# A layer with retention, attention and a squared-ReLU MLP: output rows normalised by a diagonal in their transposition, modulation's last quarter in two parts, h's second pairs at 2.5 steps per unit

## The chip, the cores and the metric

The kernel runs on one core of one Trainium2 chip. The metric is the device time in microseconds (us). The engines are TensorE (PE in the profile, its weight loads PEld), VectorE (DVE), ScalarE (ACT), GpSimd (POOL) and SyncE (SP), which here issues nearly all DMAs. Each engine runs its own instructions in order and waits for other engines by semaphores. A DMA queue is in order too: a transfer whose buffer isn't free yet holds up all that were issued behind it on that queue.

## The reference

One transformer layer over 2048 rows of 1024 (f32), with 256 rows of context. Cut to what matters here:

```
mod = silu(c) @ w_mod + b_mod                     # six parts of 1024
sh1, sc1, g1, sh2, sc2, g2 = split(mod, 6)
h  = rmsnorm(x, norm1_g) * (1 + sc1) + sh1
rq, rk, rv, rg, aq, ak, av = split(h @ w_in, ...)
ret = retention(rq, rk, rv, rg)                   # 4 heads of 128, both directions
att = attention(aq, ak, av, context)              # 8 heads of 64, 2 kv heads, 2304 keys
x  = x + g1 * (concat(ret, att) @ w_out)
h2 = rmsnorm(x, norm2_g) * (1 + sc2) + sh2
x  = x + g2 * (square(relu(h2 @ w_ff1)) @ w_ff2)  # 1024 -> 4096 -> 1024
out = rmsnorm(x, final_norm_g)
```

rmsnorm(x, g) is x · rsqrt(mean(x²) + 1e-6) · g over a row. The factor of norm2_g and 1 + sc2 is a number per column, and sh2 likewise; the factor rsqrt(...) is a number r per row.

## The kernel before, in words

**Precision.** The large products split f32 operands into a high and a low f16 part and multiply three times (high·high, high·low, low·high): one product is three MATMULs. Transpositions, modulation and parts of the retention are in f32.

**Start.** Modulation is made in four quarters, objects `mods[0]` to `mods[3]` of the class `Modulation` (L315 on): `load` fetches weights of a quarter ("wm"), `product(k)` multiplies two of its eight blocks of 128 rows (L341, in a PSUM tile "mpm" from a pool of two), `end` adds the bias on VectorE and turns the row into columns (L312, L344 to L347), and `shift_and_scale` makes the columns of sh1 and of the factor. The function `modulation(q, ...)` issues the products of a quarter with other work between them; `first.bound(k)` is a part of the first column block of w_in that needs the shifts. The order of calls is the order on PE.

**Middle.** The in-projections follow, and from about 630 us attention, written as a schedule by hand: `on(k, phase, fn)` puts a call at step k in one of eleven phases ("pe", "early", "late", "dma" and so on), and one loop issues everything in the order of step and phase. There are 32 groups of 18 steps. Per step the engines work on scores (L209, L210) and maxima (pieces L172, DVE's L185), exponentials (ACT L215), the split of the probabilities in high (ACT L219) and low parts (POOL L226 or DVE L228; tile "plo"), and values (L242 and L243). Retention (f32 matmuls at L1375, VectorE and ScalarE work) runs in between.

**Output tiles.** Sixteen tiles of 128 rows, t from 15 down to 0, one every 35 steps, each by `output_tile(t, k, last)`: transposed retention and attention results times w_out (L1497 to L1499), `add` (x + g1·product, in the tile "xr" of 128x1024), `square` (sums of squares), `store_x` (x to memory, on ScalarE's queue for t < 2), `root` (the chain of small instructions L1273 and L1274 that makes r), and three steps later `norm` (L1524): GpSimd multiplies x by r in place, 128x1024. Then, per half q of 512 columns: `transpose_x` (L1529: four PE transpositions of 128x128 into a PSUM bank), `modulate` (L1534: VectorE multiplies the bank by the column factors into a tile "u"), `shift_` (L1539: GpSimd adds sh2), `store_h` (L1542: SP stores u as half a tile of h2). The tag "u" of the pool xp has two buffers, shared with the squares' scratch; the tag "xr" has three.

The last tile, t = 0, is finished outside the schedule: its eight steps stand in the list `rest`, in the order transpose, modulate, shift, store for half 0 and then the same for half 1, and `rest_steps(n)` issues the next n of them.

**h's pairs.** h2 is read back by `h_pair(hf, j)` (L1587 to L1617), which makes seven combinations of quarters of h for a Strassen-like product, splits them in f16 parts (`form`: ACT L71 and POOL L72, into a buffer "hp") and stores them (L1607, "hf"). Each of the 14 steps first stores the form that an earlier step made. The steps are: fetch, fetch, add t1, form 0, add t2, form 5, add t3, form 1, add t4, form 3, form 2, form 6, form 4, and a last store. For the second half of the rows (hf = 1) forms with an odd number use the tag "u", those with an even number the tag "hp", two buffers each. First pairs are in the schedule of events; second pairs p0 to p3 in the feed-forward.

**Feed-forward.** From about 1590 us the work goes in units g = 4, 5, ...: seven units per block of 256 columns of w_ff1, each of 12 up-matmuls (L1706 to L1708, into PSUM tiles "pu") and, from g = 14, as many down-matmuls (L1883 to L1885). `up_out` reads the banks out (ACT L1723; DVE L1718, L1735), DVE's L1750 makes sums; these live in tiles "r" of `new_r` (eight buffers). `at(g, fn, first=...)` puts a call at a unit, in its first or its second part, and `now` issues them; within a unit the order is that in which they were put. Beside the matmuls run:
- `fetch_w1` (L1665: two loads "w1r" into the tag "xr"), sums (L1671) and forms of w1 (ACT L1683, DVE L1687);
- 16 jobs `w2_job` (loads L1809 "w2r", differences L1585, forms ACT L1819 with DVE L1828 in the tags "hp" and "u" by turns, stores L1832 "w2f"); job 1 starts at unit 4, with its b11 and b21 forms at the head of unit 6;
- the second pairs p0 to p3 at units 27, 47, 62 and 77: steps 0 and 1 at the unit itself, step k of the others at 2 + (k − 2) // 3 units later. The next job starts five units after each pair.

In units 4 to 13, `rest_steps` follows at the end of each unit: one step per unit from unit 6.

Of the kernel before, what the change touches and what calls it, by code (L numbers as in the profile page):

```python
# [11 lines left out]
F32 = mybir.dt.float32  # L12
# [5 lines left out]
ALU = mybir.AluOpType  # L18
# [4 lines left out]
P = 128  # L23
# [27 lines left out]
def bc(ap, shape):  # L51
    return ap.to_broadcast(shape)
# [3 lines left out]
def layer_kernel(ctx: ExitStack, tc: tile.TileContext, a: dict, out: bass.AP):  # L56
    nc = tc.nc
    mm = nc.tensor.matmul
# [4 lines left out]
    ident = const.tile([P, P], F32, name="ident")  # L63
# [47 lines left out]
    a2 = const.tile([P, KT], F32, name="a2")  # L111
# [155 lines left out]
    with ExitStack() as st:  # L267
# [5 lines left out]
        op = st.enter_context(tc.tile_pool(name="op", bufs=2, reuse_waits="tile"))  # L273
        sm = st.enter_context(tc.tile_pool(name="sm", bufs=3, reuse_waits="tile"))
# [19 lines left out]
        def at(q, step, fn, *args):  # L294
            plan.setdefault((q, step), []).append((fn, args))
# [190 lines left out]
        for m in range(2, len(TILES)):  # L486
            q = first_turn(m)
# [659 lines left out]
        first = weights[0]  # L1147
        mods = [Modulation(q, rows) for q in range(4)]
# [10 lines left out]
        def modulation(q, *beside):  # L1159
            for k in range(0, KT, 2):  # L1160
                mods[q].product(k)
                for fn, *args in beside[k // 2 :: 4]:
                    fn(*args)
# [14 lines left out]
        mods[1].end()  # L1178
        mods[1].shift_and_scale()
        modulation(2, (first_half, 0), (first.bound, 0), (first_half, 1), (first.bound, 2))  # L1180
        mods[2].end()
        mods[2].shift_and_scale()
        modulation(3, (first.bound, 4), (first.bound, 6))
        turn_h(0, 1)
        mods[3].end()
        mods[3].shift_and_scale()
# [30 lines left out]
    op = pool(attn, "op2", 2)  # L1217
# [4 lines left out]
    sm = pool(side, "sm2", 3, side="right")  # L1222
# [24 lines left out]
    def bank(i, shape=(P, 4, P)):  # L1247
        return psX.tile(list(shape), F32, name=f"bank{i}", tag=f"bank{i}")
# [3 lines left out]
    def on(k, phase, fn, *args):  # L1252
        events.setdefault((k, phase), []).append((fn, args))
# [202 lines left out]
    rest = []  # L1456

    def rest_steps(n):
        for _ in range(min(n, len(rest))):
            fn, *args = rest.pop(0)  # L1460
            fn(*args)
# [9 lines left out]
    def output_tile(t, k, last):  # L1471
        y = {}

        def fetch_x():
            y["x"] = xp.tile([P, D], F32, name="xr", tag="xr", bufs=3)
            nc.sync.dma_start(y["x"], a["x"][0, t * P : (t + 1) * P, :])

        def transpose(w):
            src = (rets if w == "r" else ats).pop(t)
            y["ps"] = bank(1)  # L1480
            for q in range(4):
                nc.tensor.transpose(y["ps"][:, q], src[:, q * P : (q + 1) * P], ident)

        def part(w, i):
            y[w, i] = room_tile(w + "hl"[i], F16, (P, 4, P))
            if i == 0:
                nc.scalar.activation(y[w, 0], y["ps"], AF.Copy)
            else:
                nc.vector.tensor_tensor(y[w, 1], y["ps"], y[w, 0], op=ALU.subtract)

        def product(n, k):
            if k == 0:
                y["acc", n] = bank(n if last else 0, (P, 512))
            w = "ra"[k // 4]
            hi, lo = y[w, 0][:, k % 4], y[w, 1][:, k % 4]
            wh, wl = (wo[:, k, i, n * 512 : (n + 1) * 512] for i in range(2))
            mm(y["acc", n], hi, wh, start=k == 0, stop=False)  # L1497
            mm(y["acc", n], hi, wl, start=False, stop=False)
            mm(y["acc", n], lo, wh, start=False, stop=k == KT - 1)  # L1499

        def add(n):
            c = slice(n * 512, (n + 1) * 512)
            xc = y["x"][:, c]
            nc.vector.scalar_tensor_tensor(xc, y["acc", n], sco, xc, op0=ALU.mult, op1=ALU.add)

        def square(n):
            if n == 0:
                y["ss"] = sm.tile([P, 2], F32, name="ss", tag="ss")
            c = slice(n * 512, (n + 1) * 512)
            junk = xp.tile([P, 512], F32, name="junk", tag="u")  # L1510
            nc.scalar.activation(junk, y["x"][:, c], AF.Square, accum_out=y["ss"][:, n : n + 1])

        def store_x():
            (nc.scalar if t < 2 else nc.sync).dma_start(x1_d[t], y["x"])

        def root():
            ss = y["ss"]
            chain.append(lambda: nc.vector.tensor_tensor(ss[:, :1], ss[:, :1], ss[:, 1:], op=ALU.add))
            y["r"] = rsqrt_chain(ss[:, :1], 1, 1.0 / D, "f")
            chain.append(lambda: settled.add(("f", t)))  # L1520

        def norm():
            settle(("f", t))
            nc.gpsimd.tensor_scalar(y["x"], y["x"], y["r"], 1.0, op0=ALU.mult, op1=ALU.mult)  # L1524

        def transpose_x(q):
            y["ps"] = bank(1)
            for i in range(4):
                nc.tensor.transpose(y["ps"][:, i], y["x"][:, (4 * q + i) * P : (4 * q + i + 1) * P], ident)  # L1529

        def modulate(q):
            s = slice(4 * q, 4 * q + 4)
            u = y["u", q] = xp.tile([P, 4, P], F32, name="u", tag="u")
            nc.vector.tensor_tensor(u, y["ps"], bc(a2[:, s].unsqueeze(2), [P, 4, P]), op=ALU.mult)  # L1534

        def shift_(q):
            s = slice(4 * q, 4 * q + 4)
            u = y["u", q]
            nc.gpsimd.tensor_tensor(u, u, bc(s2[:, s].unsqueeze(2), [P, 4, P]), op=ALU.add)  # L1539

        def store_h(q):
            nc.sync.dma_start(h2_d[t][:, 4 * q : 4 * q + 4], y["u", q])  # L1542

        on(k - 11, "pe", transpose, "r")
        on(k - 10, "cast", part, "r", 0)
        on(k - 9, "early", part, "r", 1)
        on(k - 6, "pe", transpose, "a")
        on(k - 5, "cast", part, "a", 0)
        on(k - 4, "early", part, "a", 1)
        on(k - 2, "dma", fetch_x)  # L1550
        places = PLACES
        if last:
            places = (-6, -5, -4, -3, 0, 1, 2, 3, -1, -1, 0, 0, 4, 5, 6, 7)
        for j, at in enumerate(places):
            on(k + at, "pe", product, j // 8, j % 8)
        on(k + places[7] + 1 + (not last), "early", add, 0)
        on(k + places[7] + 2 + (not last), "cast", square, 0)
        made = k + places[15] + 1
        on(made, "early", add, 1)
        on(made, "cast", square, 1)  # L1560
        on(made + 1, "dma", store_x)
        on(made + 1, "late", root)
        on(made + 4, "late", norm)
        if last:
            for q in range(2):
                rest.extend([(f, q) for f in (transpose_x, modulate, shift_, store_h)])
            return made, made + 5
        for q in range(2):
            at = k + (31 if t == 1 else 27) + q
            on(at, "pe", transpose_x, q)  # L1570
            on(at + 1, "early", modulate, q)
            on(at + 1, "late", shift_, q)
            on(at + 2, "dma", store_h, q)
        return made, at + 3
# [63 lines left out]
    HALF = 512  # L1638
    ff = {}
# [68 lines left out]
        mm(pu[c], wlo, hi, start=False, stop=k == 3, **more)  # L1708

    def new_r(name):  # L1710
        return ff["r"].tile([P, HALF], F32, name=name, tag="r", bufs=8)

    def up_out(b, n):
        x = rs.setdefault(b, {})
# [274 lines left out]
    with tc.manual_schedule():  # L1989
# [8 lines left out]
        for b in range(2 * NB):  # L1998
            g = 7 * b
# [12 lines left out]
        for job, g in starts.items():  # L2012
            if isinstance(job, int):
                w2_job(job, lambda k, *args: at(g + k, *args), lambda k, *args, **kw: at(g + k, *args, **kw), job >= NB - 2)
            else:
                for k, step in enumerate(h_pair(1, int(job[1]))):
                    at(g + (0 if k < 2 else 2 + (k - 2) // 3), step)
        for s in range(2 * NS):
            for n in range(7):
                at(NU * (s + 1) + 2 * n - 5, load_w2, s, n)  # L2020
# [61 lines left out]
        for g in range(4, NU * 2 * NS):  # L2082
            b, n = divmod(g, 7)
            s, u = divmod(g, NU)
            for k in range(4):
                up_part(b, n, k)
            up_out(b, n)
            if s == 0:
                now(g, True)
                now(g, False)  # L2090
                rest_steps(1 if g > 5 else 0)
                if g == NU - 1:
                    rest_steps(len(rest))
                    banks.close()
                    ff["ps2"] = pool(late_ff, "fp2", 4, space=PSUM)
                continue
            ms = (0, 1) if u % 2 == 0 else (2, 3)
            down(s - 1, u // 2, ms[0])
            now(g, True)
            down_out(s - 1, u // 2, ms[0])  # L2100
            down(s - 1, u // 2, ms[1])
            now(g, False)
            down_out(s - 1, u // 2, ms[1])
# [98 lines left out]
```

## Time and profile before

| | |
|---|---|
| Time, median of 3 runs | 2789.3 us (2785.25, 2789.3, 2796.68) |
| Profiled execution | 2786.0 us |
| Its span | 2784.2 us |
| Mean granted TensorE clock | 0.987 |
| DMA traffic | 402.51 MB, 145 GB/s over the span |
| Largest groups of instructions | L185 (DVE maxima) 390.0 us; L226 (POOL low parts) 352.4; L1706, L1707, L1708 (PE up) 341 each |

In the profile "L1529" is a line of the kernel; "out<-in" are tiles by the program's names; "[0.33 <-POOL xr L1524]" behind an instruction is the time for which its engine stood idle ahead of it, and what ended that. A row of waits, "ENGINE tile line <- RELEASER tile line: sum, times, longest", adds such idle times up. A timeline row begins with the start and the duration in us; "x4" joins four like instructions. SPq is SyncE's queue of DMA issues. A row by line gives busy us, mean ns, then idle time ahead of it. The granted clock is the share of full speed that the throttle left TensorE. One execution is profiled, and the time outside its span is 1.8 us.

### The profile page before, as it was taken

The page shows a single profiled execution, that of the slowest core. Times are in us where ns is not written, and L with a number is a line of the kernel's source. Part 1 is how long each engine was busy: PE and PEld are TensorE (multiplying, and loading weights), DVE is VectorE, ACT ScalarE, POOL GpSimd, SP SyncE. Part 2 cuts the span into 40 slices and gives each one's busy share as a digit, 9 for nine tenths or more (in the row PEclk, how much of TensorE's full clock was granted, in tenths as well). Part 3 has the DMA queues.
Part 4 walks back from the last instruction along what each step waited for, and adds up shares of the span by engine and source line. Part 5 has one row for each costly group of instructions (what it writes and reads, how often), then busy time and mean ns, then how long its engine had stood idle before and what let it go on. Part 6 is the DMA issues. An engine that isn't in the chain of part 4 may idle for free.

```text
span 2784.2 us, 44980 instructions
## 1 busy us (share of the span) xinstructions
PE 2641.8 (95%) x16768; PEld 1416.1 (51%) x16768; DVE 2096.0 (75%) x3306; ACT 1599.6 (57%) x2736; POOL 1438.0 (52%) x1182
## 2 busy tenths in 40 slices
PE   7999999887999999999899889999999999999997
PEld 3545654454666666666565434444444444444443
DVE  5857677678877777777777577988899956666676
ACT  3633762227877777777787566645554564443442
POOL 2623772465656757686767644454556721111155
PEclk8999999999999999999999999999999999999999
DMA  7478658584112222323222755665657332222223
GB/s 265 130 256 294 218 172 265 161 281 144 55 50 66 69 80 67 97 77 94 71 93 76 257 185 170 201 190 161 201 185 276 128 115 84 84 84 83 83 75 138
DMA packets 275046, 402.51 MB, mean 145 GB/s; under 512 B 107717, under 2 KB 163141, under 8 KB 272522
## 3 DMA queue, kind: packets, MB, share of 16 engines
q1 hardware_dynamic: 274538, 398.57, 44.1%
q8 instruction: 132, 2.16, 0.3%
q10 hardware_dynamic: 288, 1.05, 0.1%
q14 instruction: 88, 0.72, 0.1%
HBM read 294.54 MB, written 105.00 MB: 144 GB/s over the span
## 4 chain that ended last, share of the span: by engine, by line
PE 72%; DVE 11%; DMA 5%; ACT 4%; issue 3%; POOL 3%; SPq 1%; POOLq 0%; DVEq 0%; ACTq 0%
PE pu L1706 6%; PE pu L1707 6%; PE pu L1708 6%; PE pd L1883 6%; PE pd L1885 6%; PE pd L1884 6%; PE pso L650 5%; PE pso L651 5%; PE pso L652 5%; PE o L243 3%; PE mp L172 3%; PE st L210 3%; PE st L209 3%; DVE plo L228 2%; PE o L242 2%
## 5 line engine op out<-in xcount | busy, mean ns | idle before, releaser
L185 DVE TENSOR_REDUCE nm<-mp 128x1 f32<-128x512 f32 (+1 forms) x576 | 390.0, 684 | 161.3 <-PE mp L172 132.1
L215 ACT ACTIVATE p<-st 128x512 f32<-128x512 f32 x576 | 339.0, 599 | 173.7 <-PE st L210 105.9
L226 POOL TENSOR_TENSOR plo<-p,phi 128x1024 f16<-128x1024 f32 x160 | 352.4, 2204 | 166.4 <-ACT phi L219 136.1
L1706 PE MATMUL pu<-hf,w1f 128*128 128x512 f16 x896 | 341.5, 381 | 15.5 <-ACT w L1723 8.4
L1707 PE MATMUL pu<-hf,w1f 128*128 128x512 f16 x896 | 341.4, 381 | 0.0
L1708 PE MATMUL pu<-hf,w1f 128*128 128x512 f16 x896 | 341.1, 381 | 0.0
L219 ACT ACTIVATE phi<-p 128x1024 f16<-128x1024 f32 x288 | 304.0, 1056 | 0.0
L651 PE MATMUL pso<-wlo,h 128*128 128x512 f16 (+1 forms) x816 | 295.7, 362 | 2.0 <-DVE wlo L548 2.0
L650 PE MATMUL pso<-whi,h 128*128 128x512 f16 (+1 forms) x816 | 296.0, 363 | 1.3 <-ACT whi L547 1.3
L652 PE MATMUL pso<-whi,h 128*128 128x512 f16 (+1 forms) x816 | 295.5, 362 | 0.0
L242 PE MATMUL o<-wv,plo 128*128 128x65 f16 x2304 | 234.3, 193 | 17.0 <-POOL plo L226 10.2
L228 DVE TENSOR_TENSOR plo<-p,phi 128x512 f16<-128x512 f32 x256 | 234.6, 917 | 16.3 <-ACT phi L219 15.1
L243 PE MATMUL o<-wv,phi 128*128 128x129 f16 x2304 | 242.0, 220 | 0.0
L242 PEld LDWEIGHTS <-plo 128*128 128x128 f16 x2304 | 205.4, 98 | 61.0 <-POOL plo L226 21.3
L1909 DVE SCALAR_TENSOR_TENSOR acc<-pd,scv,acc 128x512 f32<-128x512 f32 x248 | 183.0, 742 | 55.0 <-PE pd L1885 52.3
L209 PE MATMUL st<-qr,ks 128*128 128x512 f16 x576 | 218.8, 380 | 4.9 <-ACT p L215 4.4
L210 PE MATMUL st<-qr,ks 128*128 128x512 f16 x576 | 218.9, 380 | 0.1
L243 PEld LDWEIGHTS <-phi 128*128 128x128 f16 x2304 | 204.9, 97 | 21.1 <-issue 0.3
L172 PE MATMUL mp<-ks,qr 128*128 128x512 f16 x512 | 195.5, 382 | 21.1 <-DVE nm L185 16.2
L1671 POOL TENSOR_TENSOR w1s<-w1r 128x512 f32<-128x512 f32 x64 | 91.7, 1433 | 232.7 <-ACT w L1745 153.7
L1883 PE MATMUL pd<-w2t,us 128*128 128x512 f16 x496 | 188.0, 379 | 4.4 <-DVE acc L1909 4.4
L1885 PE MATMUL pd<-w2t,us 128*128 128x512 f16 x496 | 188.0, 379 | 0.1
(377 smaller groups left out, 6083.9 us busy)
## 6 DMA issues: line engine op xcount, KB each, us to landing
w2t<-w2f SPq DMA_DIRECT2D x98, 512.0 KB, 4.2
wm<-in_w_ff SPq DMA_DIRECT2D x64, 512.0 KB, 5.0
w1r<-in_w_ff SPq DMA_DIRECT2D x64, 512.0 KB, 4.7
w2f<-w2f SPq DMA_DIRECT2D x98, 256.0 KB, 2.4
wmr<-in_w_mod SPq DMA_DIRECT2D x32, 512.0 KB, 5.2
w2r<-in_w_ff SPq DMA_DIRECT2D x32, 512.0 KB, 4.7
hf<-hp SPq DMA_DIRECT2D x56, 256.0 KB, 3.2
hf<-hf SPq DMA_DIRECT2D x14, 1024.0 KB, 7.1
```

Of the source, the lines that this page charges most:

```text
L185: nc.vector.tensor_reduce(dst, src, axis=AX.X, op=ALU.max, negate=True)
L226: nc.gpsimd.tensor_tensor(lo, p, hi, op=ALU.subtract)
L242: mm(o[:, : HD + 1], lo[:, i, c], v[:, : HD + 1], start=False, stop=False)
L243: mm(o, hi[:, i, c], v[:, :VW], start=False, stop=last)
L650: mm(self.ps[:, c], hi[:, k], wh, start=k == 0, stop=False)
L651: mm(self.ps[:, c], hi[:, k], wl, start=False, stop=False)
L652: mm(self.ps[:, c], lo[:, k], wh, start=False, stop=k == KT - 1)
L1706: mm(pu[c], whi, hi, start=first and k == 0, stop=False, **more)
L1707: mm(pu[c], whi, lo, start=False, stop=False, **more)
L1708: mm(pu[c], wlo, hi, start=False, stop=k == 3, **more)
L1883: mm(ps, uh, wh, start=first and j == 0, stop=False, **more)
L1885: mm(ps, ul, wh, start=False, stop=j == 1, **more)
```

## The change

- `norm` of the output tiles no longer scales x in place. GpSimd makes a 128x128 f32 diagonal "dg" (two buffers) that holds r, and `turn_x` replaces `transpose_x`: f32 matmuls of blocks of x with that diagonal, which transpose and scale at once.
- For the last tile, `rest` is in the order turn 0, modulate 0, turn 1, modulate 1, shift 0, store 0, shift 1, store 1; four of these steps are issued at the end of unit 5 and four at the end of unit 6. Its first turn uses bank 1 and its second bank 0.
- Products 0 and 2 of modulation's last quarter and `first.bound(4)` stand ahead of the third quarter's `end`; the other two products and `first.bound(6)` follow it.
- The second pairs' steps go 2 + (k − 2)·2 // 5 units after the pair's start. Step 7 (form 1) moves from 3 to 4 units after it, step 10 (form 2) from 4 to 5, steps 12 (form 4) and 13 (the last store) from 5 to 6; the others stay.
- Tiles "r" have seven buffers.

```diff
         modulation(2, (first_half, 0), (first.bound, 0), (first_half, 1), (first.bound, 2))
+        mods[3].product(0)
+        mods[3].product(2)
+        first.bound(4)
         mods[2].end()
         mods[2].shift_and_scale()
-        modulation(3, (first.bound, 4), (first.bound, 6))
+        mods[3].product(4)
+        mods[3].product(6)
+        first.bound(6)
         turn_h(0, 1)
...
         def norm():
             settle(("f", t))
-            nc.gpsimd.tensor_scalar(y["x"], y["x"], y["r"], 1.0, op0=ALU.mult, op1=ALU.mult)
-
-        def transpose_x(q):
-            y["ps"] = bank(1)
+            d = y["d"] = sm.tile([P, P], F32, name="dg", tag="dg", bufs=2)
+            nc.gpsimd.tensor_scalar(d, ident, y["r"], 1.0, op0=ALU.mult, op1=ALU.mult)
+
+        def turn_x(q):
+            ps = y["ps", q] = bank(1 - q if last else 1)
             for i in range(4):
-                nc.tensor.transpose(y["ps"][:, i], y["x"][:, (4 * q + i) * P : (4 * q + i + 1) * P], ident)
+                mm(ps[:, i], y["x"][:, (4 * q + i) * P : (4 * q + i + 1) * P], y["d"], start=True, stop=True)
...
-            nc.vector.tensor_tensor(u, y["ps"], bc(a2[:, s].unsqueeze(2), [P, 4, P]), op=ALU.mult)
+            nc.vector.tensor_tensor(u, y["ps", q], bc(a2[:, s].unsqueeze(2), [P, 4, P]), op=ALU.mult)
...
         if last:
-            for q in range(2):
-                rest.extend([(f, q) for f in (transpose_x, modulate, shift_, store_h)])
+            for fns in ((turn_x, modulate), (shift_, store_h)):
+                rest.extend([(f, q) for q in range(2) for f in fns])
             return made, made + 5
...
-            on(at, "pe", transpose_x, q)
+            on(at, "pe", turn_x, q)
...
-        return ff["r"].tile([P, HALF], F32, name=name, tag="r", bufs=8)
+        return ff["r"].tile([P, HALF], F32, name=name, tag="r", bufs=7)
...
-                    at(g + (0 if k < 2 else 2 + (k - 2) // 3), step)
+                    at(g + (0 if k < 2 else 2 + (k - 2) * 2 // 5), step)
...
                 now(g, True)
                 now(g, False)
-                rest_steps(1 if g > 5 else 0)
+                rest_steps(4 if g > 4 else 0)
```

## The prediction

> **What bounds the kernel now.** I read the page first: span, busy times and the chain that ended last; then the busy times by stretch of the three places that the change touches; then the waits of TensorE in them, and the timeline around each wait.
>
> ```profile
> span 2784.2 us, 44980 instructions
> PE 2641.8 (95%) x16768; PEld 1416.1 (51%) x16768; DVE 2096.0 (75%) x3306; ACT 1599.6 (57%) x2736; POOL 1438.0 (52%) x1182
> PE 72%; DVE 11%; DMA 5%; ACT 4%; issue 3%; POOL 3%; SPq 1%; POOLq 0%; DVEq 0%; ACTq 0%
> ```
>
> PE is busy 95% of the span and makes 72% of the last chain: PE work that is added costs nearly its length, unless it falls into a wait, and a wait elsewhere costs only what of it reaches PE. All of PE's idle time is 2784.2 − 2641.8 = 142 us; no rearranging can bring more.
>
> The stretches below are attention with the sixteen output tiles, the step into the feed-forward (where the last tile is finished), and a hole in the second pairs. Columns: window, its length, then busy us of PE, weight loads, DVE, ACT and POOL with counts, granted clock, DMA share, GB/s.
>
> ```profile
> 630.00:1600.00 970.00, 905.89 (x8331) 586.14 (x8331) 745.55 (x1294) 734.11 (x1202) 655.66 (x488) 0.99 0.29 92
> 1592.60:1625.20 32.60, 21.01 (x93) 9.36 (x93) 24.45 (x31) 23.05 (x40) 14.14 (x11) 0.90 0.51 164
> 1845.00:1848.40 3.40, 3.02 (x8) 1.06 (x8) 3.04 (x5) 2.29 (x4) 1.07 (x1) 0.50 0.26 65
> ```
>
> In attention PE idles 64 of 970 us (6.6%), in the 32.6 us of the step 11.6, and after the hole of 1845 the granted clock is 0.50.
>
> **A. The diagonal.** The norm on GpSimd scales 128x1024 numbers now; afterwards it makes a 128x128 diagonal, and eight f32 matmuls with it replace the tile's eight transposes: 8 x 16 = 128 instructions exchanged. The kernel has f32 matmuls of that very shape at L1375, right ahead of a block of transposes:
>
> ```profile
> L1375 PE MATMUL bank<-oqt,okt x128: 270/275/275, 695.9 to 1537.6; 128*128 128x128 f32 x128
> L1529 PE MATMUL bank<-ident,xr x128: 272/273/329, 796.1 to 1617.8; 128*128 128x128 f32 x128
> 795.25 1.05 PE L1375 MATMUL bank<-oqt,okt 128*128 128x128 f32 x8
> 796.14 0.60 PE L1529 MATMUL bank<-ident,xr 128*128 128x128 f32 x4
> 796.58 0.39 PE L234 MATMUL o<-wv,zeros 128*128 128x258 f16 x2
> ```
>
> The equal means of 273 to 275 ns mislead; the counts tell. L1375 issues 16 tiles x 4 heads = 64 matmuls and has 128 records, so an f32 matmul is two records; L1529 issues 128 transposes and has 128. By the starts, 8 records of L1375 take 796.14 − 795.25 = 0.89 us, that is 0.2225 us per matmul, and 4 transposes 796.58 − 796.14 = 0.44, or 0.110 each. The exchange adds 0.1125 x 128 = 14.4 us of PE: 13.5 in the fifteen tiles of attention, 0.9 in the last.
>
> The Trainium skill speaks against the change more strongly: "FP8 and Floating Point Precision", in its section "TensorE Precision Notes", gives a true f32 matmul four passes through the array. If a transposition takes one of them, each exchange would cost three transpositions, 42 us; L1375's two records at twice the time say 14.4, and no run here shows four.
>
> What comes back:
>
> ```profile
> L1524 POOL TENSOR_SCALAR xr<-xr,cy_f 128x1024 f32<-128x1024 f32 x16 | 21.6, 1348 | 8.7 <-DMA w2r<-in_w_ff 5.1 <-DMA x<-xr 3.6
> L1273 POOL TENSOR_SCALAR cv_f<-ss 128x1 f32<-128x1 f32 x16 | 3.1, 192 | 24.8 <-DVE ss L1518 20.6 <-PE st L210 3.0 <-PE mp L172 0.7
> PE bank L1529 <- POOL xr L1524: 4.0, 6, 1.4
> PE o L242 <- POOL plo L226: 10.2, 12, 1.7
> 1021.32 0.20 PE L242 MATMUL o<-wv,plo 128*128 128x65 f16 x1 [1.39 <-POOL plo L226]
> 1365.01 0.20 PE L242 MATMUL o<-wv,plo 128*128 128x65 f16 x1 [1.19 <-POOL plo L226]
> ```
>
> The diagonal's time lies between the 192 ns of one column and the 1348 of 1024; on the line between them 128 columns take 0.3 us, which I take. So 16 x 1.05 = 17 us of POOL come free, an engine at 655.66 of 970 there. To PE that is worth the waits on the normed tile, 4.0 us (the diagonal is ready a microsecond earlier and the largest wait was 1.4), and two of the twelve waits on the low parts, which I find directly behind a norm: 1.39 + 1.19 = 2.6. Of the added 13.5 the idle share of 6.6%, 0.9, should fall into waits. Sum: 13.5 − 4.0 − 2.6 − 0.9 = **+6**. Bounds: all twelve low-part waits go and all else as said, 13.5 − 4.0 − 10.2 = −0.7; nothing comes back, +13.5. The value is nearer the low end because the waits credited stand right behind a norm.
>
> **B. The last tile.** Its eight steps ran one per unit (a unit is 12 up-products) from unit 6; now turns and modulations of both halves come after unit 5, shifts and stores after unit 6. Its present cost, in order of time:
>
> ```profile
> 1595.82 0.38 PE L1706 MATMUL pu<-hf,w1f 128*128 128x512 f16 x1
> 1596.57 9.42 SPq L1665 DMA_DIRECT2D w1r<-in_w_ff  x2
> 1597.72 1.12 POOL L1524 TENSOR_SCALAR xr<-xr,cy_f 128x1024 f32<-128x1024 f32 x1 [5.11 <-DMA w2r<-in_w_ff]
> 1599.90 1.32 ACT L1819 ACTIVATE w2f<-w2r,scw 128x512 f16<-128x512 f32 x2
> 1602.83 0.59 ACT L1723 ACTIVATE v<-pu 128x512 f32<-128x512 f32 x1
> 1606.05 12.06 SPq L1832 DMA_DIRECT2D w2f<-w2f  x5
> 1610.44 0.72 ACT L1819 ACTIVATE w2f<-hs,scw 128x512 f16<-128x512 f32 x1 [3.49 <-DMA w2f<-w2f]
> 1611.07 0.69 DVE L1534 TENSOR_TENSOR u<-bank,a 128x512 f32<-128x512 f32 x1 [4.86 <-DMA w2f<-w2f]
> 1613.61 0.58 PE L1706 MATMUL pu<-hf,w1f 128*128 128x512 f16 x1 [6.28 <-DVE q L1750]
> 1617.17 1.48 POOL L1539 TENSOR_TENSOR u<-u,s 128x512 f32<-128x512 f32 x1
> 1625.19 0.38 PE L1706 MATMUL pu<-hf,w1f 128*128 128x512 f16 x1 [3.58 <-ACT w L1723]
> DMA to landing us min/median/max: 2.0/2.9/4.4
> ```
>
> SP's second load of w1 needs a buffer of the tag that still holds the tile's x, and stands 9.42 us at the head of the queue. The w2f stores queue behind it until 1606.05; ACT's forms and DVE's modulation wait for their buffers (3.49, 4.86), and PE for DVE: 6.28, later 3.58.
>
> Afterwards the diagonal is not held back (5.11 before the norm, which wrote x in place and so had to let x's store land), x is let go when both turns have run behind unit 5, which ends at 1595.82 (the first row is unit 6's start): eight matmuls of 0.2225 are 1.8 us, 1597.6. Then the load and the w2f stores go out. But both "u" buffers now hold modulations, and the b21 form (the second instruction of 1599.90) needs one: it waits for shift 0 and the store of half 0, which lands 2.9 us after its issue (the last line, the landing of L1542). With both modulations done by about 1598.5, the shift of 1.48 after them and the store on the queue by 1600.3, that is 1603.2. ACT reaches the form's second half at 1599.90 + 0.66 and stands from 1600.5 till then with all behind it in its queue: its own 0.66, three more instructions and then the copy out of a PE bank, which ran at 1602.83, or 2.3 after 1600.5; now it ends at about 1603.2 + 2.3 + 0.6 = 1606.1. Unit 9 waits for that bank, and unit 10, 2.6 us of matmuls and a round of DVE's sums later (I put 1.8 for three of 0.6), starts at about 1610.5 for 1613.61. The next stop, 1625.19, loses most of its own 3.58 too, since the w2f stores ahead of it went out in time; I credit 3.0 of it, so that all behind runs 6.1 earlier. Against the 0.9 of PE's exchange, 0.6 of which I charge here since PE has holes to put it in, **−5.5**. Bounds: both PE waits go, 6.28 + 3.58, less 0.9: −9; or the h store comes late, +5.7 (below).
>
> **C. The second pairs.** Steps 2 to 13 of each pair are spread over 2.5 instead of 3 per unit: forms 1 and 2 move a unit later, so do form 4 and the last store.
>
> ```profile
> ACT hp L71 <- DMA hf<-hp: 33.2, 6, 8.5
> 1737.65 0.63 ACT L71 ACTIVATE hp<-hs 128x512 f16<-128x512 f32 x1 [7.53 <-DMA hf<-hp]
> 1740.12 1.24 SPq L1809 DMA_DIRECT2D w2r<-in_w_ff  x2
> 1761.96 0.38 PE L1883 MATMUL pd<-w2t,us 128*128 128x512 f16 x1 [1.54 <-DVE acc L1909]
> 1844.21 0.63 ACT L71 ACTIVATE hp<-hs 128x512 f16<-128x512 f32 x1 [8.52 <-DMA hf<-hp]
> 1845.38 0.59 PE L1706 MATMUL pu<-hf,w1f 128*128 128x512 f16 x1 [4.16 <-ACT w L1723]
> 2028.19 0.38 PE L1883 MATMUL pd<-w2t,us 128*128 128x512 f16 x1 [0.93 <-DVE acc L1909]
> ```
>
> Form 4 writes the buffer of form 2 in the unit in which form 2's store is issued, and ACT stands until it lands: 33.2 us in six waits. PE meets 4.16 of it at 1845.38, and 1.5 more at the clock of 0.50 behind the hole (half of the 3.02 us of work there); at 1761.96 1.54, because the w2r load of the next job had queued behind the pair's last stores until 1740.12; at 2028.19 0.93. Together 8.1. Afterwards form 4 has a unit in between, and the load, five units into the pair, is issued ahead of the stores of forms 6 and 4, so these can't delay it. Form 2 comes later too, so that a fifth of this may return at the new places: **−6.5**, bounds −8.1 and 0.
>
> **D. Modulation's last quarter and the buffers.**
>
> ```profile
> 30.20 6.43 DMA wm<-in_w_mod
> 36.67 0.63 PE mpm L341 x4
> ```
>
> Two of its four products go ahead of the third quarter's sum. Its last weights land at 36.63 and PE multiplies at 36.67 by the chain: the end is set by the transfer. If that sum is set back on PE, the cover is this transfer, and without it the 0.63 of one product would be the cost: **0**, −0.5 to +0.6. Eight buffers to seven for the feed-forward's rows: by the order of the calls at most six are live, **0**.
>
> Sum: +6 − 5.5 − 6.5 + 0 = −6 on the profiled execution's 2786.0: 2780. The median of the runs shown, 2789.3, is 3.3 above that execution, so **2783** is forecast for a median.
>
> **The rivals.** *All stalls go.* The waits at 1613 and 1625 vanish (−9), the pairs' holes too (−8.1), and PE's exchange falls half into waits (+2): −15.1, 2774. For it speaks that all three are waits for a buffer that the new order frees; against it that one late thing usually uncovers the next.
>
> *The pairs' wait only moves.* ACT waits at form 2 or 6 for the stores of forms 1 and 3, C is 0 and the sum +6 − 5.5 = +0.5: 2790. For it speaks that the pair issues the same stores into the same queue.
>
> *The h store holds ACT.* This is the one on the other side. If the store of half 0 queues behind w2f stores that themselves wait, the b21 form frees ACT only at about 1610, and nine instructions of ACT (at 0.63, as at 1737.65, 5.7 us of work) follow before the banks are released: unit 9 and all behind it come 5.7 us later than before, and the sum is +6 + 5.7 − 6.5 = +5.2: 2794.5. It decides if that store lands after about 1606. For it: SP's queue is in order and stood for 12.06 us in the w2f stores; against: the h store is issued with unit 6, near the head.
>
> *Four passes.* By the time of a transposition as one pass, 0.110 x 3 x 128 = 42.2 us instead of 14.4: 27.8 more, 2811. The two records per matmul speak against it.
>
> *No effect:* that the exchange is not on PE at all can't be; it is the same array.
>
> **How the numbers follow.** Forecast 0.55; all stalls go 0.15; the wait moves 0.15; the h store holds ACT 0.12; four passes 0.03. Range 2769 to 2796: from 5 below the first rival to the third's 2794.5 and a microsecond; outside are the four passes and a few in a hundred of the others' tails. What a measurement of this kernel can tell from no change is about 0.5%, 14 us: faster means under 2775, slower over 2803. Half of the first rival and a sixth of the likeliest (A and B both near their low ends) lie under 2775: 0.08 + 0.09 = 0.17 faster. Over 2803 lie the four passes and a third of the third rival, with A at its upper bound (+13.5 + 5.7 = 19) and little from C, 0.03 + 0.04 = 0.07 slower; 0.76 within.
>
> **What would show it.** A: 256 records of the turns at L1529's place, about 0.45 us more per block of four, the norm's instruction at 0.3 us, no wait of PE on it. B: no stand of SP's w1 load from 1596, an ACT wait of 3 us on h's store near 1600, unit 10 near 1610. C: ACT's waits on hf stores down from 33.2 to under 8, no hole before 1845. D: the last product still at 36.7. I am wrong if the diagonal matmul shows four records or a block over 1 us, if ACT stands over 5 us near 1600, or if ACT's pair waits stay over 20 us.

## The result, and the profile after

The changed kernel takes 2779.17 us in the median of 7 runs (2773.42 to 2783.01), the kernel before 2792.44 beside it; the ratio is 0.9954, with a 95% interval from 0.9939 to 0.9968. That is 12.8 us less (8.9 to 17.0) where −6 was forecast. The direction holds and the time lies in the range, but the gain is twice the forecast's, and the parts show that this is not one error of scale.

The head of the page after, then the matching stretches by busy time (PE, weight loads, DVE, ACT, POOL, then granted clock):

```profile
span 2771.4 us, 45239 instructions
PE 2649.1 (96%) x16896; PEld 1430.2 (52%) x16896; DVE 2098.7 (76%) x3306; ACT 1600.1 (58%) x2736; POOL 1424.6 (51%) x1182
PE 77%; DVE 11%; DMA 3%; ACT 3%; issue 3%; POOL 2%; SPq 0%; POOLq 0%; DVEq 0%; ACTq 0%
```

```profile
630.00:1600.00 970.00, 914.95 (x8450) 600.48 (x8450) 746.52 (x1292) 733.34 (x1198) 643.54 (x489) 0.99 0.29 92
1594.00:1627.00 33.00, 25.05 (x122) 12.03 (x121) 27.54 (x36) 24.95 (x43) 14.98 (x12) 1.00 0.60 199
1835.00:1838.40 3.40, 3.40 (x17) 1.57 (x16) 3.40 (x5) 0.00 (x0) 1.23 (x1) 1.00 1.15 312
```

PE is busy 7.3 us longer and the span is 12.8 us shorter: 20 us of its idle time are gone. In the step into the feed-forward PE idles 8.0 us of 33 instead of 11.6 of 32.6 and the granted clock is 1.00 where it was 0.90; at the place of the hole (1835 after is the work of 1845 before) PE runs through.

**A after.** The turns by line, the diagonal on GpSimd by form, and the waits of PE between 653 and 1572 us, of which the first row is the kernel before, the others the one after:

```profile
L1535 PE MATMUL bank<-dg,xr x256: 272/275/377, 798.2 to 1599.5; 128*128 128x128 f32 x128
```

```profile
L1530 POOL TENSOR_SCALAR dg<-ident,cy_f 128x128 f32<-128x128 f32 x16 | 9.7, 603 | 0.2
```

```profile
PE bank L1482 <- DVE u L1534: 5.5, 11, 1.3
```

```profile
PE o L242 <- POOL plo L226: 6.7, 10, 1.7
...
PE bank L1487 <- DVE u L1540: 2.5, 6, 0.6
...
PE bank L1535 <- POOL dg L1530: 1.0, 2, 0.6
```

256 records, as forecast: two per f32 matmul. The diagonal takes 603 ns in the mean, not 300, and 9.7 us in all where the norm took 21.6, so that 12 us of GpSimd came free and not 17. PE's waits on the normed tile fell from 4.0 to 1.0 us, those on GpSimd's low parts from 10.2 to 6.7, and those of the next tile's transposition (L1482 before, L1487 after) on VectorE's modulation, which has to leave the shared bank first, from 5.5 to 2.5.

**B after.** ScalarE, then PE, then SP's queue in the step into the feed-forward:

```profile
1601.92 0.71 ACT L1825 ACTIVATE w2f<-w2r,scw 128x512 f16<-128x512 f32 x1
1606.42 0.72 ACT L1825 ACTIVATE w2f<-w2r,scw 128x512 f16<-128x512 f32 x1 [3.79 <-issue]
...
1608.75 0.58 ACT L1729 ACTIVATE v<-pu 128x512 f32<-128x512 f32 x1
...
1621.61 0.57 ACT L1729 ACTIVATE w<-pu 128x512 f32<-128x512 f32 x1
```

```profile
1597.83 1.95 PE L1535 MATMUL bank<-dg,xr 128*128 128x128 f32 x16
1599.62 0.38 PE L1712 MATMUL pu<-hf,w1f 128*128 128x512 f16 x1
...
1609.38 0.38 PE L1712 MATMUL pu<-hf,w1f 128*128 128x512 f16 x1 [1.83 <-ACT v L1729]
1613.75 0.38 PE L1712 MATMUL pu<-hf,w1f 128*128 128x512 f16 x1 [1.62 <-DVE q L1756]
1622.24 0.38 PE L1712 MATMUL pu<-hf,w1f 128*128 128x512 f16 x1 [3.14 <-ACT w L1729]
```

```profile
1599.60 0.93 SPq L1671 DMA_DIRECT2D w1r<-in_w_ff  x2
1602.35 1.33 SPq L1548 DMA_DIRECT2D h<-u  x2
1605.22 13.04 SPq L1838 DMA_DIRECT2D w2f<-w2f  x5
```

The first half of this is the forecast's sequence, 3 to 4 us later since unit 6 starts later: SP's w1 load no longer stands 9.42 us. The second of ScalarE's two forms, right behind the first before, now stands 3.79 us, until 1606.42, and the copy that unit 9 waits for follows. The profile ascribes the 3.79 to "issue" (to nothing it sees); what the form waits for follows from the two "u" buffers and the store issued at 1602.35.

The second half is not the forecast's. The w2f stores stand as long as before (13.04 us, 12.06 before), ScalarE works from 1606.42 on with a single wait of 0.56 us and comes to the next copy at 1621.61, and so PE's stop at unit 12 stays at 3.14 us, where it was 3.58. What went instead is a slow clock behind the two stops, which these stretches of the kernel before show at 0.51:

```profile
1613.60:1616.30 2.70, 2.69 (x7) 0.99 (x7) 2.70 (x5) 0.00 (x0) 0.74 (x1) 0.51 0.00 0
1626.60:1630.00 3.40, 3.40 (x10) 1.20 (x8) 2.21 (x4) 2.40 (x5) 1.77 (x2) 0.51 0.94 248
```

By these two rows it cost about 3.0 us (an estimate: 0.49 of 2.70 + 3.40); after the change the clock is 1.00 there, by the row from 1594 above. Shorter waits of PE (8.0 us instead of 11.6), the full clock (3.0) and the turns' 0.9 more of PE make up the 5.8 us that this stretch, from the first up-product of unit 4 to that of unit 14, gains.

**C after.** ScalarE around form 4 of pair p1, before and then after, and its waits on hf stores between 1700 and 2050 us, after:

```profile
1835.08 0.61 ACT L71 ACTIVATE hp<-hb 128x512 f16<-128x512 f32 x1
1844.21 0.63 ACT L71 ACTIVATE hp<-hs 128x512 f16<-128x512 f32 x1 [8.52 <-DMA hf<-hp]
1844.75 0.58 ACT L1723 ACTIVATE w<-pu 128x512 f32<-128x512 f32 x1
```

```profile
1833.06 0.60 ACT L1729 ACTIVATE w<-pu 128x512 f32<-128x512 f32 x1 [2.45 <-PE pu L1714]
...
1839.58 0.63 ACT L71 ACTIVATE hp<-hs 128x512 f16<-128x512 f32 x1 [5.32 <-DMA hf<-hp]
...
1844.01 1.33 ACT L1825 ACTIVATE w2f<-w2r,scw 128x512 f16<-128x512 f32 x2 [2.52 <-DMA hf<-hp]
```

```profile
ACT hp L71 <- DMA hf<-hp: 22.0, 6, 5.3
ACT w2f L1825 <- DMA hf<-hp: 10.4, 4, 4.3
```

ScalarE waits on hf stores almost as long as before: 22.0 + 10.4 = 32.4 us against 33.2. What changed is what stands behind the wait. Before, the copy "w<-pu" that releases a PE bank came right after form 4 and ran at 1844.75; now form 4 comes a unit later, the copy runs at 1833.06 ahead of it, and PE has its bank.

### The profile page after: what moved, and what is told of

The parts are those of the page before. It is cut to its first block, busy times and chain, and to the rows that moved or that the text cites. A ratio compares the mean times of both kernels' runs of the same rounds, so it can differ in the third digit from the quotient of the medians.

```text
span 2771.4 us, 45239 instructions
## 1 busy us (share of the span) xinstructions
PE 2649.1 (96%) x16896; PEld 1430.2 (52%) x16896; DVE 2098.7 (76%) x3306; ACT 1600.1 (58%) x2736; POOL 1424.6 (51%) x1182
## 4 chain that ended last, share of the span: by engine, by line
PE 77%; DVE 11%; DMA 3%; ACT 3%; issue 3%; POOL 2%; SPq 0%; POOLq 0%; DVEq 0%; ACTq 0%
PE pu L1712 6%; PE pu L1714 6%; PE pu L1713 6%; PE pd L1891 6%; PE pd L1889 6%; PE pd L1890 6%; PE pso L650 5%; PE pso L651 5%; PE pso L652 5%; PE o L243 3%; PE mp L172 3%; PE st L209 3%; PE st L210 3%; DVE plo L228 2%; DVE nm L185 2%
## 5 line engine op out<-in xcount | busy, mean ns | idle before, releaser
L650 PE MATMUL pso<-whi,h 128*128 128x512 f16 (+1 forms) x816 | 296.6, 363 | 1.0 <-ACT whi L547 1.0
L242 PE MATMUL o<-wv,plo 128*128 128x65 f16 x2304 | 233.8, 193 | 14.4 <-DVE plo L228 7.4
L228 DVE TENSOR_TENSOR plo<-p,phi 128x512 f16<-128x512 f32 x256 | 235.0, 919 | 15.6 <-ACT phi L219 14.4
L242 PEld LDWEIGHTS <-plo 128*128 128x128 f16 x2304 | 205.4, 98 | 56.0 <-POOL plo L226 15.6
```

What stands on the lines that cost most here:

```text
L242: mm(o[:, : HD + 1], lo[:, i, c], v[:, : HD + 1], start=False, stop=False)
L650: mm(self.ps[:, c], hi[:, k], wh, start=k == 0, stop=False)
```

## The experiments

The theory after the comparison: A costs about nothing, since the turns' longer PE work falls into waits; B is worth about what was forecast; C is worth more, though its wait stays. The rival is the forecast's own account (A +6, B −5.5, C −6.5). All ratios are to the kernel before, run beside; in us they are taken on 2792.

**Each part by itself, and all but A's fifteen tiles.** a_only is the changed kernel with modulation, pairs, the order of `rest` and its steps set back; b_only has modulation and pairs set back and the diagonal in the last tile alone; no_diag_above_0 is the changed kernel with the diagonal in the last tile alone:

```diff
 # a_only (from the changed kernel; modulation not shown)
-            ps = y["ps", q] = bank(1 - q if last else 1)
+            ps = y["ps", q] = bank(1)
...
-            for fns in ((turn_x, modulate), (shift_, store_h)):
-                rest.extend([(f, q) for q in range(2) for f in fns])
+            for q in range(2):
+                rest.extend([(f, q) for f in (turn_x, modulate, shift_, store_h)])
...
-                    at(g + (0 if k < 2 else 2 + (k - 2) * 2 // 5), step)
+                    at(g + (0 if k < 2 else 2 + (k - 2) // 3), step)
...
-                rest_steps(4 if g > 4 else 0)
+                rest_steps(1 if g > 5 else 0)
 # b_only and no_diag_above_0: norm and turn_x by tile
+            if not last:
+                nc.gpsimd.tensor_scalar(y["x"], y["x"], y["r"], 1.0, op0=ALU.mult, op1=ALU.mult)
+                return
...
+                if not last:
+                    nc.tensor.transpose(ps[:, i], y["x"][:, (4 * q + i) * P : (4 * q + i + 1) * P], ident)
+                    continue
 # c_only: the kernel before with
-                    at(g + (0 if k < 2 else 2 + (k - 2) // 3), step)
+                    at(g + (0 if k < 2 else 2 + (k - 2) * 2 // 5), step)
```

> The kernel before with the diagonal in all sixteen tiles, the last tile's steps and everything else in the old order (seven buffers r make room for the diagonal). The forecast: 14.4 us more of PE, 8 us of waits back, +6 to +7 us. The rival, read from the two traces by the shift of like matmuls between 640 and 1595 us: +4 or less, because more waits shrink than those right behind the norm. A third: nothing comes back, +14. Records of the turn: 256 by all three.

Measured: 0.9995 (0.9986 to 1.0004), −1.4 us (−3.9 to +1.1). The forecast's +6 is refuted; the rival's "+4 or less" holds, with +4 itself outside.

> The kernel before with the new order of the last tile and the diagonal in that tile alone; the other fifteen tiles are scaled and transposed as before, modulation and pairs as before. The forecast: -5.5 us. The rival, from the shift of the up-products between units 6 and 12 of the two traces: -7.5, half a clock's stretch at 1613 going too. That only the whole change gains: 0.

Measured: 0.9991 (0.9982 to 1.0001), −2.5 us (−5.0 to +0.3). In its trace the stretch from the first up-product of unit 4 to that of unit 14 is 4.6 us shorter than in the profile before, which is near the forecast. The time doesn't confirm that it all reaches the end: −5.5 lies just outside the interval, −7.5 is out, and 0 is not excluded.

> The kernel before with the second pairs at 2.5 steps per unit and nothing else. The forecast: -6.5 us, with ScalarE's waits on hf stores between 1700 and 2050 us falling from 33 to under 8. The rival, from the traces: -9 us though ScalarE still waits about 30 us on hf stores, because each wait now ends before PE needs ScalarE. That C's gain depends on the earlier shift by B: under 3 us.

Measured: 0.9971 (0.9962 to 0.998), −8.1 us (−10.6 to −5.6). C is the largest part, and by itself. Its trace has the same waits of ScalarE on hf stores as the changed kernel:

```profile
ACT hp L71 <- DMA hf<-hp: 23.5, 7, 4.6
ACT w2f L1819 <- DMA hf<-hp: 10.5, 3, 4.9
```

So the gain doesn't come from the wait becoming shorter; the rival of −9 had that right.

> The changed kernel with the fifteen tiles t > 0 scaled in place and transposed as before; the last tile keeps diagonal and order, pairs and modulation as changed. The forecast: 6 us faster than the changed kernel, so -19 us against before by the measured -13. The rival: A costs 4 or less, -14 to -17. That freeing GpSimd is worth more than the matmuls cost: slower than the changed kernel, -10 or less.

Measured: 0.996 (0.9945 to 0.9975), −11.2 us (−15.4 to −7.0), beside −12.8 (−17.0 to −8.9) with the diagonal everywhere. The forecast's −19 is outside. Within what is measured, some 6 us to each side, fifteen tiles' diagonals cost nothing and bring nothing.

**The order or the diagonal in the last tile.** b_transposes has the new order with scaling in place and transpositions in every tile, modulation and pairs set back as in b_only (in part, against the changed kernel):

```diff
-            d = y["d"] = sm.tile([P, P], F32, name="dg", tag="dg", bufs=2)
-            nc.gpsimd.tensor_scalar(d, ident, y["r"], 1.0, op0=ALU.mult, op1=ALU.mult)
+            nc.gpsimd.tensor_scalar(y["x"], y["x"], y["r"], 1.0, op0=ALU.mult, op1=ALU.mult)
...
-                mm(ps[:, i], y["x"][:, (4 * q + i) * P : (4 * q + i + 1) * P], y["d"], start=True, stop=True)
+                nc.tensor.transpose(ps[:, i], y["x"][:, (4 * q + i) * P : (4 * q + i + 1) * P], ident)
```

> The kernel before with the new order of the last tile, but scaled in place and transposed as before in all tiles. If the order alone carries B: -2 to -5 us. If the diagonal carries it, because scaling in place has to wait until the store of x has landed and PE's turns, now behind unit 5 instead of 6, wait with it: a wait of PE of about 3 us on GpSimd near 1596 us, and 0 to +3 in all.

Measured: 0.9994 (0.9985 to 1.0003), −1.7 us (−4.2 to +0.8), not told apart from b_only by time. The trace shows the wait that was expected, so the diagonal does its part in B:

```profile
1608.28 1.09 PE L1529 MATMUL bank<-ident,xr 128*128 128x128 f32 x8 [2.77 <-POOL xr L1524]
```

The same stretch from unit 4 to unit 14 took 42.3 to 43.7 us in the four profiles that have this part as before (before, c_only, c_form4, d_only), 39.9 here, 39.3 in a_only, with the diagonal in the old order, and 36.4 to 37.9 in the five profiles with both: order and diagonal each gain some. The profile before is the shortest of its four.

**Why A costs nothing.** Three kernels take its two sides apart. a_twice issues every diagonal matmul twice; no_norm has no scaling at all (the transpositions as before); turns_twice issues every transposition of the kernel before twice.

```diff
 # a_twice (from a_only)
+                for _ in range(2):
                     mm(ps[:, i], y["x"][:, (4 * q + i) * P : (4 * q + i + 1) * P], y["d"], start=True, stop=True)
 # no_norm (from the kernel before)
-            nc.gpsimd.tensor_scalar(y["x"], y["x"], y["r"], 1.0, op0=ALU.mult, op1=ALU.mult)
 # turns_twice (from the kernel before)
+                for _ in range(2):
                     nc.tensor.transpose(y["ps"][:, i], y["x"][:, (4 * q + i) * P : (4 * q + i + 1) * P], ident)
```

> The diagonal in all tiles in the old order, with every one of its matmuls issued twice (the second overwrites the first): 14.4 us of PE work more than the diagonal alone, which ran at -1.4 us against before. If PE is the bound and what came back with the diagonal came from GpSimd's 12 us less work: +12 to +14. If attention has slack that takes up PE work wherever it stands: +5 or less.

Measured: 1.0079 (1.0067 to 1.0092), +22.1 us (18.7 to 25.7). The expectation's arithmetic was wrong: doubling adds a whole f32 matmul, 128 x 0.2225 = 28.5 us, not the 14.4 of the exchange. Against a_only it is 23.5 more, so 8 tenths of these 28.5 show in the time. Slack that takes up any PE work is refuted.

> The kernel before without the scaling of the sixteen tiles; transpositions as before. It leaves out the factor r of norm2. It shows what the freed GpSimd is worth without PE's price. The forecast's credits: -6.6 to -7.5 us in attention. The traces' (waits of PE on low parts, on the bank behind the modulation and on the scaled tile): -10, and about -3 more in the last tile. Only the waits on the scaled tile itself: -4.

Measured: 0.9982 (0.9972 to 0.9991), −5.0 us (−7.8 to −2.5). The freed GpSimd is worth some 5 us, not 10. Its waits of PE say why:

```profile
PE bank L1482 <- DVE u L1533: 6.9, 11, 1.1
...
PE o L242 <- POOL plo L226: 6.5, 9, 1.7
...
PE bank L1528 <- DVE u L1533: 3.6, 5, 1.9
```

The low parts' row falls to 6.5, as with the diagonal. But a PE that comes to the turn earlier waits longer for VectorE to leave the bank: 6.9 + 3.6 = 10.5 us, where the kernel with the diagonal waits 2.5 + 0.4.

> The kernel before with each transposition of the normed tiles issued twice into the same place: 128 more of 0.110 us, 14.1 us of PE work exactly where the diagonal's matmuls add theirs, with GpSimd's scaling left as it was. If the waits of PE on VectorE's modulation that follow the turns (5.5 us, 11 times, before; 2.5 with the diagonal) take up a good part of it: +6 to +9, and that row falls to under 3 us. If PE work there costs its length less the idle share, as the forecast had it: +13. If all that the diagonal brought back came from GpSimd: +14.

Measured: 1.0016 (1.0006 to 1.0026), +4.5 us (1.7 to 7.3), for 14.1 us of added PE work. Of these, 9.6 are absorbed (6.8 to 12.4): two thirds, a little more than the theory had said. The row that was named falls from 5.5 to 1.3:

```profile
PE o L242 <- POOL plo L226: 8.2, 11, 1.7
...
PE bank L1482 <- DVE u L1535: 1.3, 3, 0.8
```

Of the 9.6, these two rows show 4.2 behind VectorE and 2.0 on the low parts (10.2 before); where the rest went they don't show.

So the account of A is: +14.4 on PE; about −5 for GpSimd (no_norm); about −10 for PE work that falls into waits which stand at that place anyway, those for VectorE first (turns_twice: 14.1 − 4.5). That comes to about 0, if the two may be added, and −1.4 (−3.9 to +1.1) was measured. The second helping of PE work (a_twice) finds that row for VectorE gone and shows nearly whole.

**What of C's edit counts.** c_form4 moves only form 4 and the last store.

```diff
-                    at(g + (0 if k < 2 else 2 + (k - 2) // 3), step)
+                    at(g + (0 if k < 2 else 2 + (k - 2) // 3 + (k > 11)), step)
```

> The kernel before with steps 12 and 13 of the second pairs (form 4 and the last store) a unit later, and forms 1 and 2 where they were. If the unit between form 2 and form 4 carries C, as the forecast had it: -6 to -9 us, ScalarE's waits on hf stores near 0 for form 4. If forms 1 and 2 must move too (their stores crowd the queue): -4 or less.

Measured: 0.997 (0.9959 to 0.9981), −8.4 us (−11.4 to −5.3): all of C, so the unit that form 4 moves carries it. But not for the forecast's reason, that form 2's store has landed by then, since form 4 still waits:

```profile
ACT hp L71 <- DMA hf<-hp: 20.0, 5, 5.2
ACT w2f L1819 <- DMA hf<-hp: 8.9, 3, 5.4
```

The traces say it more sharply than the times. From the first up-product of unit 25 to that of unit 95 all six profiles with C or with form 4's shift alone take 362.6 us, the eight without 371.3 to 374.5.

**D, and a version that might be better.** d_only moves the modulation's products alone. halves is no_diag_above_0 with the scaling of t > 0 in two pieces of 512 columns, a step apart; after_again is the changed kernel on the same chip.

```diff
 # halves (the transpositions as in no_diag_above_0)
-        def norm():
+        def norm(q=0):
...
+            if not last:
+                c = slice(q * 512, (q + 1) * 512)
+                nc.gpsimd.tensor_scalar(y["x"][:, c], y["x"][:, c], y["r"], 1.0, op0=ALU.mult, op1=ALU.mult)
+                return
...
+        if not last:
+            on(made + 5, "late", norm, 1)
```

> The kernel before with modulation's last quarter in two parts and nothing else. The forecast: 0 (-0.5 to +0.6), last product of the modulation between 36.4 and 37.2 us. The rival: the half-clock stretch after PE's 3 us wait at 32 goes, -1 to -2.

Measured: 0.9996 (0.9986 to 1.0005), −1.1 us (−3.9 to +1.4): no difference that can be told. The last of modulation's matmuls starts at 37.5 us in its trace, at 36.9 before and at 36.3 after, within the 36.3 to 38.1 of all fourteen profiles.

> The changed kernel with the fifteen tiles t > 0 transposed as before, but scaled in two halves of 512 columns, the second a step later, so that GpSimd's low parts wait for half a scaling at most; the last tile with the diagonal. If the low parts' waits behind the scaling (10.2 us before, 6.5 with the diagonal) come from its 1.35 us at one piece: that row falls to 6 to 8 us, and the kernel is 2 to 4 us faster than with whole scaling, -13 to -15 against before. If not: -11, as with whole scaling.

Measured: 0.9942 (0.9928 to 0.9956), −16.2 us (−20.1 to −12.3).

> The changed kernel as it is, beside the others on one chip: -13 against before, as measured; the variant in halves is better if it lies below by more than the interval.

Measured: 0.995 (0.9938 to 0.9963), −14.0 us (−17.3 to −10.3). The variant in halves has the lowest median of all, 2775.98 beside 2778.89, and −11, as with whole scaling, is outside its interval. But that interval overlaps with the changed kernel's, and its reason failed: the low parts' row is

```profile
PE o L242 <- POOL plo L226: 9.5, 16, 1.7
```

instead of 6 to 8. Whether halves are better than the diagonal stays open.

## Why the prediction was right in its sign and half in its size

**A's price was right, its rebate was not.** Two records per f32 matmul, 14.4 us of PE, about 0.45 more per block: all as forecast. The named rebates were about right too: 4.0 forecast and 3.0 seen on the scaled tile, 2.6 and 3.5 on the low parts. The step that failed is "the idle share of 6.6%, 0.9, should fall into waits". A mean over 970 us was used for a place with waits of its own: right behind the turns PE waited 5.5 us for VectorE, in a row of the same view from which the rebates were taken. Work at that place is absorbed by two thirds (turns_twice), not by 6.6%. With that, +6 becomes about 0; the measured −1.4 (−3.9 to +1.1) lies by its middle even below the forecast's own bound of −0.7, which counted waits for GpSimd alone.

The rival of four passes failed on its premise. Twelve f16 up-products of 512 columns start within 2.37 us, 0.215 apart, which makes 0.054 per 128 columns (an estimate by their length):

```profile
1595.25 0.38 PE L1712 MATMUL pu<-hf,w1f 128*128 128x512 f16 x1 [0.69 <-ACT w L1729]
...
1597.62 0.38 PE L1714 MATMUL pu<-hf,w1f 128*128 128x512 f16 x1
```

The f32 matmul's 0.2225 is about four of these. The Trainium skill ("FP8 and Floating Point Precision", "TensorE Precision Notes") gives a true f32 matmul four passes through the array, and the trace agrees. But the f32 transposition's 0.110 is two of them and not one, so the exchange costs 14.4 us and not 42.

**B's first step was right, its second was not.** The diagonal is not held back, SP's load is free, and ScalarE is held by half 0's store: 3 us forecast, 3.79 in the first profile, 3.4 to 5.3 in the five with the new order and the diagonal (over 5, the prediction's sign of being wrong, in two of them). The step that failed is "loses most of its own 3.58 too, since the w2f stores ahead of it went out in time; I credit 3.0 of it": the stores stand 13.04 us, and the stop keeps 3.14. Counted from unit 4, unit 10 comes 1.9 us earlier where the forecast has 3.1. That the whole stretch still gains 5.8 in the first profile, beside −5.5, is luck: the slow clock behind the two stops, about 3.0, went too, a term that the forecast counted behind the hole of 1845 but not here. By the time of b_only B is −2.5 (−5.0 to +0.3), and whether this or the trace's 5.8 is nearer to what B is worth stays open. Part of what I credited to the order is the diagonal's alone (3.0 in a_only). The rival in which h's store holds ScalarE to 1610 had the right wait, without the w2f stores ahead of it.

**C's size was near, its mechanism wrong.** −8.1 measured for −6.5 with bounds −8.1 and 0; by the stretch from unit 25 to unit 95, 8.9 in the first pair of profiles and at least 8.7 in any, somewhat over that bound. The failed step is that "ACT's waits on hf stores" would go "from 33.2 to under 8"; they stayed at 32. The prediction itself named over 20 us there as a sign that it is wrong, and in this point it is. It had asked how long form 4 waits, where the question was what is queued behind it: a bank's copy before, nothing urgent after. Hence the fifth that it kept back for "new places" was not lost either: in the changed kernel's profile PE has none of the holes at 1761, 1845 and 2028. The rival "the pairs' wait only moves" had the wait right and drew the wrong end from it.

**D** can't be told from 0, as forecast. The seven buffers have no run of their own; a_only and b_only have them, and neither is slower than before.

By the parts alone the sum is −1.4 − 2.5 − 8.1 − 1.1 = −13.1, beside −12.8 for the whole: the parts add up, and no interplay is needed. Each part is known to some 2.5 us, so the sum is no closer than about 5. Of the 7 us between forecast and measurement nearly all is A by these numbers (7.4); B's 3 too many and C's 1.6 and D's 1.1 too few make up for each other. That B, C and D together come out near their forecast is thus in part luck.

## What to carry to other kernels

Price added work by the waits that end right behind the place where it stands, not by the engine's mean idle share, and look whether the engine that it waits for there would be late anyway. When a wait is moved, ask what is queued behind the waiting instruction: the wait need not become shorter, it only must no longer stand ahead of the instruction that the busiest engine needs. When a stop goes, ask what clock PE had behind it. Where several parts are changed at once, time each by itself: a forecast whose sum is near can hold one part 7 us too dear.

## What the runs showed that was not expected

The same instructions take different times from one execution to the next. The in-projections, from the first to the last product of L650, took 579.9 us in the profile of before and 580.9 to 586.5 in the other thirteen profiles, which have the same instructions there; attention, from the first to the last product of L242, took 904.0 to 910.3 us in the seven profiles whose output tiles before the last are those of before (905.1 to 907.0 in after, after_again and a_only, 901.4 in no_norm, 927.9 in a_twice). So one profile can't price a part of 5 us that is spread over attention, and the profile that the forecast started from was the quickest of the fourteen in the first of these stretches. A hole at a fixed place is a firmer thing: the one of p1 stands in PE's row at unit 54 in all eight profiles without C (3.5 to 4.9 us), and in the six with it PE has no wait over 0.3 us between units 25 and 95.

The diagonal's instruction on GpSimd varies by more than threefold (shortest, median and longest ns behind the count, after):

```profile
L1530 POOL TENSOR_SCALAR dg<-ident,cy_f x16: 370/396/1324, 795.0 to 1594.7; 128x128 f32<-128x128 f32 x16
```

Its median, 396, is near the 300 that the line from one column to 1024 gave; a few long ones make the mean of 603.
